# Six weight buffers spread over offsets modulo 128 bytes in SBUF

## The chip, the cores and the metric

The kernel runs on one core of a Trainium2 chip. The metric is the device time of one execution in microseconds. The time before is a median of 919.14 us over three runs (918.66 to 919.76).

## The reference, cut to what matters

The kernel computes one layer of a streaming-encoder block in float32 for 512 tokens of width 1024: a combined input projection, sliding-window attention, gated linear attention, a gated mix, cross-attention to 256 memory tokens, and a SwiGLU feed-forward block of inner width 2816.

```python
h = _rms(x, norm_mix_w)
proj = h @ w_in                      # attention q, k, v; GLA q, k, v, g, gate rank; branch gates
...
merged = g_a * (o_a @ w_attn_o) + g_b * (o_g @ w_gla_o)
x = x + merged @ w_mix_o
x = x + _memory_xattn(_rms(x, norm_mem_q_w), _rms(mem, norm_mem_kv_w), w_mem_q, w_mem_kv, w_mem_o)
x = x + (silu(hf @ w_gate) * (hf @ w_up)) @ w_down      # hf = _rms(x, norm_ffn_w)
out = _rms(x, norm_final_w)
```

What costs time is matrix products with weights of 83 MB in all, which are read from HBM once.

## The kernel before, in words

Every weight matrix comes in units of 128 partitions by up to 1024 columns of float32. `unit` (line 110) loads a unit by a DMA on SP's queue into a tile R, and `split` (line 95) makes two tiles of it: the upper part H, by a cast on ACT (line 97), and the lower part L = R - H, by a subtraction on DVE (line 98). Each of R, H and L has three buffers of 4096 bytes a partition, which take turns from unit to unit, so there are three for the upper and three for the lower part. Activations stand in the same way as pairs `xh`, `xl` (`weighted`, line 231), `oh`, `ol`, `mh`, `ml`, `ah`, `al` and so on, each 512 columns, 2048 bytes a partition.

A product is taken as three matmuls (`prod3`, line 122): H with `xh`, H with `xl`, L with `xh`. Two loops do nearly all of them:

- `block` (line 125): a piece of 128 columns (512 bytes a partition) of H or L is the stationary operand, and 512 tokens of an activation are the moving one. All gates, queries, output projections and the whole feed-forward part go this way. A unit gives eight pieces, so 24 matmuls.
- `tokens` and `token_terms` (lines 257 and 268): 128 tokens of an activation are stationary and a slice of H or L moves. It is 512 columns wide for the GLA's values and gates, and 328 for the columns of `w_tg` (TGW, line 31), with two slices in one unit; the second of these begins 328 x 4 = 1312 bytes into the tile, which is 32 modulo 128.

In the profile a matmul is named output<-moving,stationary, so `mm<-xh,H` is one of `block` and `mm<-H,xh` one of `token_terms`.

Tiles are placed in pools that fill SBUF from the left and the right end. The tile `edge` (line 50) is 96 bytes of padding at the right end. With it, H, L, R and all activation tiles begin at 0 modulo 128 bytes; some small tiles (`ident`, `ones`, `alr`, norm scalars) do not. The pool `wp` of R, H and L is the second from the left, behind `cp`, which holds the constants.

A scheduler sets the order of instructions on each engine from dependences and its own estimates of durations; in the attention part PE's order is written out by hand. Engines work through their rows in order, and semaphores tie them together. At the start, the first projection is computed while x arrives chunk by chunk: `load`, `chunk` and `keys` (lines 294 to 302) bring a chunk of x, make `xh` (ACT) and `xl` (DVE) of it and multiply it with the keys' weights (tile `o`), and `Norm.add` squares it (ACT, `sq`) and sums it (DVE, `acc_n`, line 205). `Norm.finish` then multiplies `acc_n` with `ones` on PE (`t<-ones,acc_n`).

Of the kernel before, what the change touches and what calls it, by code (L numbers as in the profile page):

```python
# [11 lines left out]
F32 = mybir.dt.float32  # L12
F32R = mybir.dt.float32r
# [7 lines left out]
P = 128  # L21
# [13 lines left out]
def build(tc, a, out):  # L35
# [3 lines left out]
    def pool(name, bufs=1, side=None, space=None):  # L39
        kw = {"name": name, "bufs": bufs, "reuse_waits": "tile"}  # L40
        if side is not None:
            kw["side"] = side
        if space is not None:
            kw["space"] = space
        return tc.tile_pool(**kw)

    cp = ctx.enter_context(pool("cp"))
# [3 lines left out]
    wp = ctx.enter_context(pool("wp"))  # L51
# [7 lines left out]
    def uniq(s):  # L59
        names[0] += 1  # L60
        return f"{s}_{names[0]}"
# [41 lines left out]
            )  # L103

    def unit_tiles():
        return [
            wp.tile([P, 1024], dt, tag=tag, bufs=3, name=uniq(tag)) for tag, dt in (("R", F32), ("H", F32R), ("L", F32R))
        ]

    def unit(src):  # L110
        n = src.shape[-1]
        r, h, lo = unit_tiles()
        nc.sync.dma_start(r[:, :n], src)
        split(h[:, :n], lo[:, :n], r[:, :n])
        return h, lo
# [34 lines left out]
    nc.gpsimd.memset(edge, 0.0)  # L150
    ident = cp.tile([P, P], F32, name="ident")
    make_identity(nc, ident)
    ones = cp.tile([P, P], F32, name="ones")
    nc.gpsimd.memset(ones, 1.0)

    def small(name, shape, src):
# [74 lines left out]
    def weighted(x, w, k):  # L231

        h = xwp.tile([P, S], F32R, tag="xw", bufs=16, name=uniq("xh"))
        lo = xwp.tile([P, S], F32R, tag="xw", bufs=16, name=uniq("xl"))
        split(h, lo, x, w[:, k : k + 1])
        return h, lo
# [495 lines left out]
    for t in range(NT):  # L732
# [9 lines left out]
        r = cp.tile([P, 4], F32, name=f"rr{t}")  # L742
# [43 lines left out]
    for j in range(KC):  # L786
# [7 lines left out]
        h = mg2.tile([P, S], F32R, name=f"mh{j}")  # L794
        lo = mg2.tile([P, S], F32R, name=f"ml{j}")
# [11 lines left out]
    for k in range(KC):  # L807
        if k % 2 == 0:
            two = f(xwp.tile([P, S], F32R, tag="xw", bufs=16, name=uniq("mem")))
        r = two[:, (k % 2) * NM : (k % 2 + 1) * NM]  # L810
# [5 lines left out]
    for k in range(KC):  # L816
# [3 lines left out]
        h = mep.tile([P, NM], F32R, name=f"eh{k}")  # L820
        lo = mep.tile([P, NM], F32R, name=f"el{k}")
# [8 lines left out]
    for j in range(KC):  # L830
# [6 lines left out]
        h, lo = weighted(x, wq_w, j)  # L837
# [151 lines left out]
    for u in range(2):  # L989
        h4, l4 = unit(a["w_mem_o"][u])  # L990
        for i in range(4):
# [9 lines left out]
            h, lo = weighted(res[j], wf_w, j)  # L1001
# [132 lines left out]
```

## Time and profile before

| | |
|---|---|
| median of three runs | 919.14 us |
| the profiled execution, its own time | 919.91 us |
| its span, first to last instruction | 918.1 us |
| PE busy | 901.2 us, 98% |
| DVE busy | 557.4 us, 61% |
| ACT busy | 426.5 us, 46% |
| granted TensorE clock, mean | 0.995 |

The record of a matmul with 512 columns is about 390 ns long, and in the feed-forward part the next one starts 227 ns after it, so records overlap. So the busy share says that PE is never empty, and not how fast it goes. The pace is read from the starts of matmuls that follow one another. [...]

### The profile page before, as it was taken

The numbers are of one execution on the slowest core, as the hardware profiler recorded it, in microseconds if no ns is written. First come the engines' busy times: TensorE is split into PE (matmuls) and PEld (weight loads), VectorE is DVE, ScalarE is ACT, GpSimd is POOL, SyncE is SP. The second block draws the span as 40 slices with busy tenths as digits, with TensorE's granted clock in tenths as the row PEclk, the third lists the DMA queues.
The fourth block names the chain that finished last, engine by engine and source line by source line (L and its number), as shares of the span: only waits on it lengthen the run. The fifth ranks groups of instructions, "written<-read, shape, count | busy, mean of one in ns | idle before, by whom it ended". The sixth has DMA issues, their size and how long they took to land.

```text
span 918.1 us, 11424 instructions
## 1 busy us (share of the span) xinstructions
PE 901.2 (98%) x4318; PEld 746.7 (81%) x4318; DVE 557.4 (61%) x1104; ACT 426.5 (46%) x760; POOL 7.0 (1%) x30
## 2 busy tenths in 40 slices
PE   8999999999999999999999999999999999999995
PEld 6898888887888787778888778888888888888885
DVE  6777888777343959966766996444444444323323
ACT  7576574556333838463445864223332233222220
POOL 1000000000000000000000000000000000000001
PEclk9999999999999999999999999999999999999998
DMA  7232221222232031425432222232222322323212
GB/s 249 92 115 70 69 70 69 70 69 69 92 96 89 23 115 48 143 86 161 114 115 92 70 89 95 94 107 99 92 92 92 106 100 86 104 86 103 87 41 92
DMA packets 29415, 86.11 MB, mean 94 GB/s; under 512 B 4048, under 2 KB 7760, under 8 KB 29360
## 3 DMA queue, kind: packets, MB, share of 16 engines
q1 hardware_dynamic: 29216, 85.37, 28.9%
q8 instruction: 34, 0.56, 0.2%
q14 instruction: 21, 0.17, 0.1%
q10 hardware_dynamic: 144, 0.00, 0.0%
HBM read 83.27 MB, written 2.10 MB: 93 GB/s over the span
## 4 chain that ended last, share of the span: by engine, by line
PE 89%; DVE 6%; ACT 3%; DMA 1%; issue 1%; SPq 0%; DVEq 0%; ACTq 0%
PE mm L79 80%; PE s L79 3%; PE o L79 3%; PE t L79 1%; DVE L L98 1%; PE t L545 1%; ACT pm L93 1%; DMA R<-in_w_tg 1%; PE mm L545 1%; ACT H L97 1%; DVE sl L98 1%; DVE on L747 1%; DMA x<-in_xT 0%; PE t L758 0%; DVE st L706 0%
## 5 line engine op out<-in xcount | busy, mean ns | idle before, releaser
L97 ACT CAST H<-R 128x1024 fp32r<-128x1024 f32 (+2 forms) x155 | 156.8, 1013 | 326.1 <-PE mm L79 247.0
L98 DVE TENSOR_TENSOR L<-R,H 128x1024 fp32r<-128x1024 f32 (+2 forms) x155 | 181.8, 1174 | 93.9 <-ACT H L97 93.5
L79 PE MATMUL mm<-xl,H 128*128 128x512 f32 x592 | 232.3, 392 | 0.0
L79 PE MATMUL mm<-xh,L 128*128 128x512 f32 x592 | 232.1, 392 | 0.0
L79 PE MATMUL mm<-xh,H 128*128 128x512 f32 x592 | 230.6, 390 | 0.0
L79 PEld LDWEIGHTS mm<-xh,H 128*128 128x128 f32 x592 | 111.2, 188 | 22.5
L79 PEld LDWEIGHTS mm<-xl,H 128*128 128x128 f32 x592 | 111.2, 188 | 22.1
L79 PEld LDWEIGHTS mm<-xh,L 128*128 128x128 f32 x592 | 111.3, 188 | 21.7
L79 PE MATMUL mm<-ah,H 128*128 128x512 f32 (+1 forms) x198 | 72.5, 366 | 0.0
L79 PE MATMUL mm<-ah,L 128*128 128x512 f32 (+1 forms) x198 | 72.4, 366 | 0.0
L79 PE MATMUL mm<-al,H 128*128 128x512 f32 (+1 forms) x198 | 72.4, 365 | 0.0
L79 PE MATMUL mm<-H,xh 128*128 128x512 f32 (+1 forms) x192 | 70.3, 367 | 0.0
L79 PE MATMUL mm<-L,xh 128*128 128x512 f32 (+1 forms) x192 | 70.3, 366 | 0.0
L79 PE MATMUL mm<-H,xl 128*128 128x512 f32 (+1 forms) x192 | 70.1, 365 | 0.0
L1024 DVE TENSOR_TENSOR t2k<-t2k,mm 128x512 f32<-128x512 f32 x22 | 15.0, 687 | 68.3 <-PE mm L79 67.7
L93 ACT ACTIVATE p<-sm,nm,sc 128x256 f32<-128x256 f32 (+1 forms) x64 | 36.3, 569 | 25.4 <-DVE es L519 20.3
L1022 DVE TENSOR_TENSOR t2k<-mm,rb_n 128x512 f32<-128x512 f32 x22 | 15.1, 691 | 44.9 <-PE mm L79 43.0
L79 PEld LDWEIGHTS mm<-al,H 128*128 128x128 f32 x198 | 37.3, 189 | 6.1
L79 PEld LDWEIGHTS mm<-ah,H 128*128 128x128 f32 x198 | 37.3, 189 | 6.0
L79 PEld LDWEIGHTS mm<-ah,L 128*128 128x128 f32 x198 | 37.3, 189 | 6.0
L79 PEld LDWEIGHTS mm<-L,xh 128*128 128x128 f32 x192 | 36.1, 188 | 5.5 <-DVE L L98 0.6
L79 PEld LDWEIGHTS mm<-H,xh 128*128 128x128 f32 x192 | 36.3, 189 | 5.1 <-issue 0.2
(300 smaller groups left out, 1365.7 us busy)
## 6 DMA issues: line engine op xcount, KB each, us to landing
R<-in_w_fg SPq DMA_DIRECT2D x22, 512.0 KB, 3.2
R<-in_w_fu SPq DMA_DIRECT2D x22, 512.0 KB, 3.3
R<-in_w_gate SPq DMA_DIRECT2D x16, 512.0 KB, 3.3
R<-in_w_fd SPq DMA_DIRECT2D x16, 512.0 KB, 3.5
x<-in_xT SPq DMA_DIRECT2D x16, 256.0 KB, 3.5
R<-in_w_q SPq DMA_DIRECT2D x8, 512.0 KB, 3.5
R<-in_w_attn_o SPq DMA_DIRECT2D x8, 512.0 KB, 3.3
R<-in_w_vg SPq DMA_DIRECT2D x8, 512.0 KB, 3.3
```

Of the source, the lines that this page charges most:

```text
L79: nc.tensor.matmul(o, lhsT=lhsT, rhs=rhs, start=start, stop=stop)
L93: last_table[0] = nc.scalar.activation(*args, **kw)
L97: nc.scalar.copy(out=hi, in_=src)
L98: nc.vector.tensor_tensor(out=lo, in0=src, in1=f(hi), op=ALU.subtract)
L545: nc.tensor.transpose(out=pt[:, i * P : (i + 1) * P], in_=prs[i // 2][:, i % 2, b * P : (b + 1) * P], identity=ident)
L747: nc.vector.scalar_tensor_tensor(out=on[t][:, vs], in0=on[t][:, vs], scalar=r[:, h : h + 1], in1=glaw, op0=ALU.mult, op1=ALU.mult)
L1022: nc.vector.tensor_tensor(out=t, in0=pg, in1=n2.b, op=ALU.mult)
L1024: nc.vector.tensor_tensor(out=t, in0=t, in1=pu, op=ALU.mult)
```

## The change

```diff
     def unit_tiles():
-        return [
-            wp.tile([P, 1024], dt, tag=tag, bufs=3, name=uniq(tag)) for tag, dt in (("R", F32), ("H", F32R), ("L", F32R))
-        ]
+        r = wp.tile([P, 1024], F32, tag="R", bufs=3, name=uniq("R"))
+        i = wturn[0] = (wturn[0] + 1) % 3
+        h = wp.tile([P, 1024 + 8], F32R, tag=f"H{i}", bufs=1, name=uniq("H"))
+        lo = wp.tile([P, 1024 + (24 if i == 2 else 8)], F32R, tag=f"L{i}", bufs=1, name=uniq("L"))
+        return r, h[:, 8:1032], lo[:, 8:1032]
+
+    wturn = [-1]
...
-    ones = cp.tile([P, P], F32, name="ones")
+    ones = cp.tile([P, 32], F32, name="ones")
```

Each H and L tile gets 8 columns (32 bytes) more in front, and its data begin behind them. The tiles lie one behind the other as H0, L0, H1, L1, H2, L2, each 4128 bytes long (32 x 128 + 32) but the last, which is 4192. So they begin at 0, 32, 64, 96, 0 and 32 modulo 128, and their data at 32, 64, 96, 0, 32 and 64. Together they are 256 bytes longer than before, which is twice 128; `ones` is 384 bytes shorter, three times 128. So every other tile keeps its offset modulo 128. R is as it was. The three buffers of each part take turns as before, and every wait on a buffer stays; only two columns of `ones` were ever read.

No instruction is added or removed. Its memset being shorter, `ones` shifts the scheduler's estimates on POOL a little, and some rows at the kernel's start change places; after the first projection all rows stand as before on every engine. ACT at the start, where x's chunks 4 to 7 (`x_4` to `x_7`) and the last two units of `w_tg` and the second half of `w_k` (`R_214`) arrive, before:

```order
L97 CAST H_215<-R_214 128x512
L100 ACTIVATE xh_257<-x_4_81,wk 128x512
L199 ACTIVATE sq_278<-x_4_81 128x512
L100 ACTIVATE xh_262<-x_5_82,wk 128x512
L97 CAST H_267<-R_266 128x656
L100 ACTIVATE xh_285<-x_6_83,wk 128x512
L199 ACTIVATE sq_281<-x_5_82 128x512
L97 CAST H_295<-R_294 128x656
L100 ACTIVATE xh_290<-x_7_84,wk 128x512
```

ACT at the same place, now:

```order
L100 ACTIVATE xh_257<-x_4_81,wk 128x512
L97 CAST H_215<-R_214 128x512
L100 ACTIVATE xh_262<-x_5_82,wk 128x512
L204 ACTIVATE sq_278<-x_4_81 128x512
L97 CAST H_267<-R_266 128x656
L100 ACTIVATE xh_285<-x_6_83,wk 128x512
L204 ACTIVATE sq_281<-x_5_82 128x512
L100 ACTIVATE xh_290<-x_7_84,wk 128x512
L97 CAST H_295<-R_294 128x656
```

Two casts of weights have gone behind a chunk of x, and one square behind a chunk. DVE follows, before:

```order
L98 TENSOR_TENSOR L_216<-R_214,H_215 128x512
L101 SCALAR_TENSOR_TENSOR xl_258<-x_4_81,wk,xh_257 128x512
L205 TENSOR_TENSOR acc_n_124<-acc_n_124,sq_278 128x512
L101 SCALAR_TENSOR_TENSOR xl_263<-x_5_82,wk,xh_262 128x512
L98 TENSOR_TENSOR L_268<-R_266,H_267 128x656
L205 TENSOR_TENSOR acc_n_124<-acc_n_124,sq_281 128x512
L101 SCALAR_TENSOR_TENSOR xl_286<-x_6_83,wk,xh_285 128x512
L98 TENSOR_TENSOR L_296<-R_294,H_295 128x656
L101 SCALAR_TENSOR_TENSOR xl_291<-x_7_84,wk,xh_290 128x512
L205 TENSOR_TENSOR acc_n_124<-acc_n_124,sq_306 128x512
```

and now:

```order
L101 SCALAR_TENSOR_TENSOR xl_258<-x_4_81,wk,xh_257 128x512
L98 TENSOR_TENSOR L_216<-R_214,H_215 128x512
L101 SCALAR_TENSOR_TENSOR xl_263<-x_5_82,wk,xh_262 128x512
L210 TENSOR_TENSOR acc_n_124<-acc_n_124,sq_278 128x512
L98 TENSOR_TENSOR L_268<-R_266,H_267 128x656
L101 SCALAR_TENSOR_TENSOR xl_286<-x_6_83,wk,xh_285 128x512
L210 TENSOR_TENSOR acc_n_124<-acc_n_124,sq_281 128x512
L101 SCALAR_TENSOR_TENSOR xl_291<-x_7_84,wk,xh_290 128x512
L98 TENSOR_TENSOR L_296<-R_294,H_295 128x656
L210 TENSOR_TENSOR acc_n_124<-acc_n_124,sq_306 128x512
```

`xl` now stands ahead of the sum `acc_n` and of the lower parts beside it. On PE the three rows `mm_126<-H_267,xh_257`, `mm_126<-H_267,xl_258` and `mm_126<-L_268,xh_257` have gone behind the last two of the keys, `o_125<-xl_291,H_215` and `o_125<-xh_290,L_216`. SP's rows, the DMAs, stand as before.

## Rows read from the trace of the kernel before

**Rows 1.** The profile's page: busy time of each engine, and the chain's shares by engine.

```profile
PE 901.2 (98%) x4318; PEld 746.7 (81%) x4318; DVE 557.4 (61%) x1104; ACT 426.5 (46%) x760; POOL 7.0 (1%) x30
...
PE 89%; DVE 6%; ACT 3%; DMA 1%; issue 1%; SPq 0%; DVEq 0%; ACTq 0%
```

**Rows 2.** The chain that ended last: start us, length us, engine, line, count.

```profile
563.52 333.00 PE mm L79 x1500
```

**Rows 3.** Two stretches: length, busy us and count by engine, granted clock, DMA share, GB/s.

```profile
60.00:240.00 180.00, 180.00 (x904) 149.19 (x903) 139.48 (x400) 110.68 (x251) 0.32 (x1) 1.00 0.23 76
...
565.00:885.00 320.00, 320.00 (x1413) 265.08 (x1412) 134.31 (x158) 96.37 (x118) 0.00 (x0) 1.00 0.30 94
```

**Rows 4.** Timeline in the feed-forward part: start us, length us, engine, line, operation.

```profile
600.13 0.39 PE L79 MATMUL mm<-xh,H 128*128 128x512 f32 x1
...
600.37 1.22 DVE L98 TENSOR_TENSOR L<-R,H 128x1024 fp32r<-128x1024 f32 x1
...
604.22 1.06 ACT L97 CAST H<-R 128x1024 fp32r<-128x1024 f32 x1 [3.11 <-PE mm L79]
...
605.57 0.39 PE L79 MATMUL mm<-xh,H 128*128 128x512 f32 x1
```

**Rows 5.** PE's groups by form: line, operation, count, busy us, mean ns, idle before.

```profile
L79 PE MATMUL mm<-xh,H 128*128 128x512 f32 x592 | 230.6, 390 | 0.0
L79 PE MATMUL mm<-ah,H 128*128 128x512 f32 x154 | 59.9, 389 | 0.0
...
L79 PE MATMUL mm<-H,xh 128*128 128x512 f32 x128 | 50.3, 393 | 0.0
...
L79 PE MATMUL mm<-ogh,H 128*128 128x512 f32 x64 | 24.5, 394 | 0.0
...
L79 PE MATMUL mm<-H,xh 128*128 128x328 f32 x64 | 20.0, 314 | 0.0
```

**Rows 6.** Timeline of token_terms over w_tg: every third matmul, H or L moving.

```profile
48.62 0.31 PE L79 MATMUL mm<-H,xh 128*128 128x328 f32 x1
...
49.08 0.31 PE L79 MATMUL mm<-H,xh 128*128 128x328 f32 x1
...
49.52 0.31 PE L79 MATMUL mm<-H,xh 128*128 128x328 f32 x1
...
49.97 0.31 PE L79 MATMUL mm<-H,xh 128*128 128x328 f32 x1
...
50.42 0.31 PE L79 MATMUL mm<-H,xh 128*128 128x328 f32 x1
```

**Rows 7.** Timeline of the last product, 256 columns wide: two matmuls with 23 between.

```profile
889.04 0.28 PE L79 MATMUL mm<-ah,L 128*128 128x256 f32 x1
...
891.92 0.28 PE L79 MATMUL mm<-ah,L 128*128 128x256 f32 x1
```

**Rows 8.** DVE's and ACT's largest groups by form, columns as in rows 5.

```profile
L98 DVE TENSOR_TENSOR L<-R,H 128x1024 fp32r<-128x1024 f32 x136 | 166.1, 1222 | 89.1 <-ACT H L97 88.7
...
L97 ACT CAST H<-R 128x1024 fp32r<-128x1024 f32 x136 | 142.8, 1052 | 295.2 <-PE mm L79 223.3 <-issue 71.6
```

**Rows 9.** DMA issues from 0 to 30 us: count, KB each, us to landing.

```profile
x<-in_xT SPq DMA_DIRECT2D x8, 256.0 KB, 4.4
```

**Rows 10.** Timeline of the kernel's start.

```profile
8.50 0.90 SPq L295 DMA_DIRECT2D x<-in_xT  x2
...
12.29 0.62 ACT L97 CAST H<-R 128x512 fp32r<-128x512 f32 x1 [1.15 <-DMA R<-in_w_k]
...
17.24 0.74 ACT L97 CAST H<-R 128x656 fp32r<-128x656 f32 x1 [0.25 <-DMA R<-in_w_tg]
...
18.44 0.50 PE L79 MATMUL o<-xl,H 128*128 128x512 f32 x1 [0.92 <-DVE xl L101]
...
21.10 0.69 DVE L205 TENSOR_TENSOR acc_n<-acc_n,sq 128x512 f32<-128x512 f32 x1 [0.47 <-ACT sq L199]
...
21.94 1.02 PE L79 MATMUL t<-ones,acc_n 128*128 128x2 f32 x8
```

## The prediction, made before the changed kernel ran

> **What bounds the kernel now.** I read the page first: PE is busy for 901.2 of 918.1 us, and the chain that ended last is 89% PE [rows 1]. The chain's longest piece is 333.00 us of matmuls without a break [rows 2]. So the kernel is as fast as PE steps from one matmul to the next, and DVE and ACT matter only where PE waits for them.
>
> The pace is read next. In the feed-forward part two matmuls `mm<-xh,H` start at 600.13 and 605.57; 24 steps lie between them, as one unit of weights has 24 matmuls, so a step is 5.44 / 24 = 226.7 ns [rows 4]. The whole stretch says the same: 1413 matmuls in 320.00 us are 226.5 ns each, at a granted clock of 1.00, which is the 2.4 GHz level [rows 3]. At that clock 512 columns take 512 / 2.4 = 213.3 ns. So each step is 13.3 ns, or 32 column times, longer than its columns. Two other widths show the same excess: twelve steps of 328 columns take 50.42 - 48.62 = 1.80 us, 150.0 ns each [rows 6], where the columns take 136.7; and 24 steps of 256 columns take 2.88 us, 120.0 ns each [rows 7], where they take 106.7. What these 13.3 ns are, no row says. They are the only thing on the path that a buffer's place could change, and that is the whole question.
>
> **The change part by part.** Nothing is added or removed, so each item is a change of duration or of order. *H and L as stationary operands* (`block`). The rows count 592 + 154 + 3 x 64 groups of three matmuls with 512 moving columns (`ogh` in the row; `oh` and `mh` have as many) [rows 5], so 2814 steps. The moving tiles stay at 0 modulo 128 bytes. The pieces of H and L are 512 bytes long, so all pieces of one tile have their tile's offset: 0 in all of them before, and now 32 and 96 for two thirds and one third of H, 64 and 0 for L. Three causes for the 13.3 ns can be told apart by what the offset does: a fixed cost of changing weights (nothing), a collision of the weight load with the moving stream in a bank that is chosen by the low address bits (a change of either sign), and a cost for rows that begin off a boundary (a loss). The trace of before holds one natural experiment on it, the next item.
>
> *H and L as moving operands* (`token_terms`). Of the 328-column slices every second one begins at 32 modulo 128, against a stationary operand at 0. In [rows 6] the slices alternate: three steps from 48.62 and three from 49.52 are at offset 0 and take 0.46 + 0.45 = 0.91 us, the three from 49.08 and from 49.97 are at offset 32 and take 0.44 + 0.45 = 0.89 us. That is 151.7 against 148.3 ns a step, which is one printed digit, and the twelve together take exactly 12 x 150.0, that is columns plus 32, just as the widths whose operands all lie at 0. If offset 32 paid, the sum should have come out below; if it cost, above. I read it as no effect, with a bound of 1.7 ns a step (half of the difference) on either side. A distance of 32 bytes between the two operands also covers H1 as a stationary operand (weights at 96, stream at 0), and L1 stays at 0. Distances of 64 (L0, L2) and 96 (H0, H2) are in no row that is paced by columns. By the two seen I take 0 for them too, and the bound goes into the rivals. Sum: 0 us.
>
> *DVE and ACT.* `L<-R,H` takes 1222 ns and `H<-R` 1052 ns [rows 8]. In the feed-forward part DVE is busy for 134.31 and ACT for 96.37 of 320 us [rows 3], so per unit (5.44 us) for 2.3 and 1.6 us. If each subtraction took half as long again, 0.6 us more, the 3.1 us of slack would hide it. In the attention part (60 to 240 us) DVE is busy for 139.48 of 180 us and 904 matmuls run [rows 3], at 24 a unit no more than 38 units; 0.6 us each would be 23 us of the 40 us that DVE has free there. Also, neither engine gains anything for the end if it gets faster. 0 us.
>
> *The start.* Here rows change places. ACT took the keys' last unit at 12.29, having waited 1.15 us for it to land, and `x_4` behind it [rows 10]. Now `x_4` comes first. It was issued at 8.50 [rows 10], and chunks of x land after 4.4 us [rows 9], so at about 12.9; ACT then starts 12.9 - 12.29 = 0.6 us later than before, and the sums `acc_n` behind it on DVE by up to as much. Some of it comes back, since ACT had 0.25 us of waiting before the last cast of `w_tg` [rows 10]. On the other side, `xl` of chunk 6 now stands ahead of a sum, and PE's 0.92 us of waiting for it at 18.44 shrinks. But that gain ends at the next wait: `t<-ones,acc_n` started at 21.94, and the last sum ended at 21.79 (21.10 + 0.69) [rows 10], so PE can't go through there more than 0.1 us earlier whatever it saves ahead of it. Between -0.1 and +0.6 us; I take +0.3, as the landing that moved is the nearer row. The smaller memset of `ones` lies on POOL, which is busy for 7.0 us in all [rows 1], and is hidden.
>
> Sum: the profiled execution's 919.91 us (span 918.1 and 1.8 around it) + 0 + 0 + 0.3 = 920.2. That execution was 0.8 above the median of 919.14, and the result will be a median, so 919.4 us.
>
> **The rivals.** *Faster: the 13.3 ns are a collision that the equal offsets make.* Weights and stream are read at the same time, and now both begin at the same place modulo 128. Moving the weights to 32, 64 and 96 would free the stream. For it: the excess is the same for 256, 328 and 512 columns, as it would be if each weight load cost a fixed number of reads. Against it: offset 32 in [rows 6]. At the bound from there it gives 1.7 ns for 2814 + 3 x 128 = 3198 steps of 512 columns [rows 5], so 5.4 us: 914.0. If the whole excess went it would be 42.6 us: 877. [...] Chance 0.16.
>
> *Slower: a moving row that begins off a 128-byte boundary costs one piece more.* 2048 bytes at offset 0 are 16 pieces of 128 bytes, and at 32, 64 or 96 they touch 17. 32 columns of 4 bytes are just 128 bytes, so the price of a piece would be one more 13.3 ns. It falls in `token_terms` over the GLA's values and gates: 384 steps [rows 5], of which eight ninths use a buffer off 0 (H in two of three matmuls, always off 0; L in one, off 0 in two of three buffers), so 341 x 13.3 = 4.5 us: 923.9. For it: the 328-column rows say nothing on it, as 1312 bytes touch 11 pieces at offset 0 and at 32. It decides from half a piece on. Against it: no row shows any price of an offset. As stationary operands the pieces are covered, the weight loads being busy for 265.08 of 320 us [rows 3] beside the stream. [...] Collisions at the unseen distances of 64 and 96 would end on this side as well; they concern two thirds of 3198 steps, and 1.7 ns each are 3.6 us: 923.0. Chance of both 0.18.
>
> *The change doesn't do what it says.* Sizes and paddings add up to the offsets named, and the tiles around keep theirs, so only if the real granule were larger than 128 bytes would all stay alike; that gives 919.4 too, and is part of the forecast.
>
> **How the numbers follow.** No measurable change has 0.66, faster 0.16, slower 0.18. About 0.2%, or 1.8 us, is what a measurement of this kernel can tell from no change; the start alone, -0.1 to +0.6 us, stays inside. The likeliest case alone reaches from 918.0 to 921.0, by the spread of the three runs and the start. The range goes to the prices of the two rivals at their bounds, 914.0 and 923.9, which holds the forecast and about half of each rival, 0.83.
>
> **What would show it.** If I am right, the step in the feed-forward part stays at 226.7 ns in all three turns of the buffers, and the 328-column steps at 150.0. The faster rival would show as a shorter step in units of some buffers, repeating every three units; the slower one as a step of about 240 ns for `mm<-H,xh` with 512 columns, with `block` unchanged. In the start, `t<-ones,acc_n` should come between 21.8 and 22.5. I would be wrong above all if the pace depends on a distance of 64 or 96 bytes, on which the trace has no row.

## The result, and the profile after

The changed kernel takes 932.75 us, the median of four runs (932.18 to 933.45), against 919.21 us for the kernel before on the same chip. The ratio is 1.0148, with a 95% interval of 1.0130 to 1.0165. So it is slower by 13.5 us, where I forecast 919.4 us and no measurable change; the time lies above the whole range (914.0 to 923.9).

The profiled execution of the changed kernel took 932.18 us, its span is 930.4 us, and its mean granted clock 0.996 (0.995 before). From its page, the busy times and the chain's shares by engine:

```profile
PE 915.1 (98%) x4318; PEld 746.5 (80%) x4318; DVE 556.9 (60%) x1104; ACT 425.8 (46%) x760; POOL 6.8 (1%) x30
...
PE 92%; DVE 3%; ACT 2%; DMA 1%; issue 1%; SPq 0%; DVEq 0%; ACTq 0%
```

PE is busy for 13.9 us more than in [rows 1] with the same 4318 matmuls, DVE and ACT are as they were, and the chain has moved from DVE and ACT to PE. So PE did not wait longer: its work became longer. The stretch 565 to 885 us by windows (us, then PE, PEld, DVE, ACT, POOL busy with counts, granted clock, DMA share, GB/s) says how:

```profile
565.00:885.00 320.00, 319.94 (x1385) 258.88 (x1385) 134.13 (x165) 93.61 (x114) 0.00 (x0) 1.00 0.28 93
```

PE is full and at the same clock as in [rows 3], but 1385 matmuls start in 320 us instead of 1413: 231.0 ns a step instead of 226.5. The chain's pieces (start, length, engine, line, count), of the changed kernel:

```profile
228.72 73.00 PE mm L79 x313
...
569.19 340.48 PE mm L79 x1500
```

and the piece of the kernel before that answers to the first of them:

```profile
227.66 71.18 PE mm L79 x313
```

The long feed-forward piece of [rows 2] has grown from 333.00 to 340.48 us, so by 7.5 of the 12.3 us that the span grew; the piece of 313 matmuls ahead of it by 1.8. The rest lies in other stages. The timeline shows that the loss goes by buffers. These are four first matmuls of a unit, 24 steps apart, with the buffer that H has in turn: 0, 1, 2, and 0 again.

```profile
599.67 0.39 PE L79 MATMUL mm<-xh,H 128*128 128x512 f32 x1
...
605.22 0.39 PE L79 MATMUL mm<-xh,H 128*128 128x512 f32 x1
...
610.77 0.39 PE L79 MATMUL mm<-xh,H 128*128 128x512 f32 x1
...
616.37 0.39 PE L79 MATMUL mm<-xh,H 128*128 128x512 f32 x1
```

A unit takes 5.55, 5.55 and 5.60 us, where [rows 4] had 5.44, and the next three take the same again. That is 231.3, 231.3 and 233.3 ns a step. One more thing can be read here. H0 and H2, and L0 and L2, lie at the same offsets modulo 128 (32 and 64), yet their units differ by 2 ns a step. So what counts is not the place modulo 128 alone.

### The profile page after: what moved, and what is told of

Its sections match the earlier page's. It is cut to its first block, busy times and chain, and to the rows that moved or that the text cites. A ratio compares the mean times of both kernels' runs of the same rounds, so it can differ in the third digit from the quotient of the medians.

```text
span 930.4 us, 11424 instructions
## 1 busy us (share of the span) xinstructions
PE 915.1 (98%) x4318; PEld 746.5 (80%) x4318; DVE 556.9 (60%) x1104; ACT 425.8 (46%) x760; POOL 6.8 (1%) x30
## 4 chain that ended last, share of the span: by engine, by line
PE 92%; DVE 3%; ACT 2%; DMA 1%; issue 1%; SPq 0%; DVEq 0%; ACTq 0%
PE mm L79 83%; PE o L79 3%; PE s L79 3%; PE t L79 1%; PE t L550 1%; ACT pm L93 1%; PE mm L550 1%; DMA x<-in_xT 1%; DVE L L98 0%; DMA R<-in_w_k 0%; PE t L763 0%; ACT H L97 0%; DVE sl L98 0%; ACT th L97 0%; DVE mkl L260 0%
## 5 line engine op out<-in xcount | busy, mean ns | idle before, releaser
L79 PE MATMUL mm<-xh,L 128*128 128x512 f32 x592 | 234.9, 397 | 0.0
L79 PE MATMUL mm<-xh,H 128*128 128x512 f32 x592 | 233.1, 394 | 0.0
```

The lines of the kernel that those rows point to most:

```text
L79: nc.tensor.matmul(o, lhsT=lhsT, rhs=rhs, start=start, stop=stop)
```

## Experiments

Three causes were open: the distance in bytes between the two operands that PE reads; a start off a boundary as such; and something else that the change moved (the order at the start, the tiles of activations on either side). In all that follows, *distance* is the address of the stationary operand's piece less that of the moving one. For the kernel and its variants it is that of `block`, where the weights are stationary.

**1. The changed layout with H and L put back to 0.** The order at the start and the shift of the left-hand tiles stay.

```diff
-        h = wp.tile([P, 1024 + 8], F32R, tag=f"H{i}", bufs=1, name=uniq("H"))
-        lo = wp.tile([P, 1024 + (24 if i == 2 else 8)], F32R, tag=f"L{i}", bufs=1, name=uniq("L"))
-        return r, h[:, 8:1032], lo[:, 8:1032]
+        h = wp.tile([P, 1024], F32R, tag=f"H{i}", bufs=1, name=uniq("H"))
+        lo = wp.tile([P, 1024 + (64 if i == 2 else 0)], F32R, tag=f"L{i}", bufs=1, name=uniq("L"))
+        return r, h, lo[:, 0:1024]
```

> The changed kernel with its order of rows and its places of all other tiles, but H and L themselves at 0 modulo 128 again (256 bytes of padding stand behind L2). H and L are now 256 or 384 bytes (modulo 512) away from the activations, instead of 0. Theory 1, distance: a step's time depends on the distance in bytes between the start of the moving stream and the start of the weights that are loaded beside it, and a distance of 0 is the good one. If only the distance modulo 128 counts, 919 us and a step of 226.7 ns in the feed-forward part; if a larger modulus counts, slower, up to 932.8. Theory 2, boundary: an operand that starts off a 128-byte boundary costs more: 919 us. Theory 3, something else that the change moved (the rows at the start, the other tiles by 128 and 384 bytes): 932.8 us and steps of 231 to 233 ns.

It took 921.29 us, 1.0023 times the kernel before (1.0014 to 1.0033). The changed order is not the cause. The chain's pieces:

```profile
226.73 72.18 PE mm L79 x313
...
564.65 332.97 PE mm L79 x1500
```

The feed-forward piece is back at 333 us. The small loss of 2 us has a place: the piece of 313 matmuls, 72.18 us against 71.18, and one of 153, 35.60 against 34.79, where `oh` and `ogh` are multiplied; the mean step of the 153 is 35.60 / 153 = 232.7 ns, where it was 227.4. The change shifts the tiles on the left by 128 bytes, weights included, and not those on the right. `oh`, `ogh` and `omh` stand on the right, so 432 steps have a distance of 128 here where they had 0. About 2 us over 432 steps is 5 ns each, much as the steps of the changed kernel pay. Multiples of 128 are not all alike.

**2. Everything at 32.** The kernel before, with 32 bytes put ahead of `wp` and the padding at the right end made 32 bytes shorter, so that weights and activations all lie at 32 modulo 128, at distance 0.

```diff
-    edge = ctx.enter_context(pool("ep", side="right")).tile([P, 24], F32, name="edge")
+    edge = ctx.enter_context(pool("ep", side="right")).tile([P, 16], F32, name="edge")
+    shift = ctx.enter_context(pool("shp")).tile([P, 8], F32, name="shift")
...
+    nc.gpsimd.memset(shift, 0.0)
```

> The kernel before, with every tile behind the constants, H, L, R and all activations, 32 bytes further: every operand starts at 32 modulo 128, and all distances stay 0. Theory 1, distance: 919 us, a step of 226.7 ns. Theory 2, boundary: slower; with one price per operand off a boundary at least as slow as the changed kernel (932.8 us), in which only H and L are off. Theory 3 has no reason for a change: 919 us.

It took 919.39 us, ratio 1.0003 (0.9993 to 1.0013), and its feed-forward piece 332.99 us. A start off a boundary costs nothing by itself. Only the distance is left.

**3. The distance alone.** A kernel that leaves the whole block out: PE runs 24 matmuls for each setting, at chosen offsets of weights (`st`) and stream (`mv`), and its output is a copy of x. From 30 to 330 us no DVE or ACT instruction runs, and DMA moves 1 GB/s. The loop, simplified to its float32 settings:

```python
def run(name, s, m, cols=512, ...):        # s, m: offsets of weights and stream in bytes
    for i in range(24):
        st = w[:, s // 4 + i // 3 * P : s // 4 + i // 3 * P + P]
        mv = xs[i // 3][:, m // 4 : m // 4 + cols]
        nc.tensor.matmul(o[:, :cols], lhsT=st, rhs=mv, ...)
```

> Not the block of the reference: PE alone, with nothing else running, does 24 matmuls with 24 weight loads per setting, and the output is a copy of x. The settings: the stationary operand 0 to 496 bytes from a 512-byte boundary in steps of 16 (and 4, 8, 12) with the stream at 0 (st); the stream at 32 to 480 in steps of 32 with the weights at 0 (mv); both at the same offset (both); 32, 64 and 96 stationary columns instead of 128 at offsets 0 and 32 (w); 256 moving columns (c256); bf16 operands (bfst). Theory 1, distance: 226.7 ns a step at st0 and in all of both, 229 to 236 at other distances, and mv at an offset the same as st at minus that offset. Theory 2, boundary: both as slow as st and mv. If the excess of 32 columns over the 512 comes from the reads of the weight load, it shrinks with the stationary columns (8, 16 and 24 at 32, 64 and 96) and is smaller for bf16, which has half the bytes; if it is a fixed price of changing weights, it stays 13.3 ns at any width. If steps at some distance take less than 226.7 ns, there is a kernel that beats both.

From its timeline, one row for each setting (start, length, engine, line, operation, output<-moving,stationary, count); the step is the time to the next row's start, divided by 24. Starts are printed to 0.01 us, so a step read in this way is good to about 0.4 ns:

```profile
26.57 5.60 PE L58 MATMUL st0x<-x,w 128*128 128x512 f32 x24
32.01 5.61 PE L58 MATMUL st16x<-x,w 128*128 128x512 f32 x24
37.46 5.75 PE L58 MATMUL st32x<-x,w 128*128 128x512 f32 x24
43.05 5.76 PE L58 MATMUL st48x<-x,w 128*128 128x512 f32 x24
...
93.33 5.66 PE L58 MATMUL st192x<-x,w 128*128 128x512 f32 x24
98.82 5.76 PE L58 MATMUL st208x<-x,w 128*128 128x512 f32 x24
...
110.02 5.62 PE L58 MATMUL st240x<-x,w 128*128 128x512 f32 x24
115.48 5.60 PE L58 MATMUL st256x<-x,w 128*128 128x512 f32 x24
120.92 5.61 PE L58 MATMUL st272x<-x,w 128*128 128x512 f32 x24
...
204.38 5.77 PE L58 MATMUL mv32x<-x,w 128*128 128x512 f32 x24
209.99 5.67 PE L58 MATMUL mv64x<-x,w 128*128 128x512 f32 x24
...
288.12 5.62 PE L58 MATMUL both32x<-x,w 128*128 128x512 f32 x24
293.57 5.64 PE L58 MATMUL both64x<-x,w 128*128 128x512 f32 x24
...
309.99 5.71 PE L58 MATMUL w32st0x<-x,w 128*32 128x512 f32 x24
315.53 5.87 PE L58 MATMUL w32st32x<-x,w 128*32 128x512 f32 x24
...
359.88 5.34 PE L58 MATMUL bfst32x<-xb,wb 128*128 128x512 bf16 x24
365.06 5.34 PE L58 MATMUL bfst64x<-xb,wb 128*128 128x512 bf16 x23
370.24 5.34 PE L58 MATMUL bfst96x<-xb,wb 128*128 128x512 bf16 x24
```

At distance 0 a step is 5.44 / 24 = 226.7 ns, the kernel's own pace, and at 16 it is 227.1. At 32 it is 5.59 / 24 = 232.9 ns, and it stays between 231.7 and 234.2 up to 160. At 176 it is 230.0, at 192 228.8, at 208 and 224 again 233.3, and at 240 (227.5) and 256 (226.7) the cheap place has come back. The second half, up to 496, repeats the first, so the period is 256 bytes. Moving the stream instead costs as much (`mv32x`, 233.8 ns), and the sign counts: with the stream moved by 64 the step is 229.2 ns, the sweep's at 192 and not its 232.9 at 64. Moving both by 32 costs nothing (227.1). So PE alone pays for the distance between its two operands, modulo 256, and no other engine or DMA is needed for it. With bfloat16 a step is 5.18 / 24 = 215.8 ns at 32 and at 64, and at 0 it is 216.3 (5.19 us). Fewer stationary columns do not make the step shorter: with 32 of them it is 230.8 ns at distance 0, with 64 and with 96 it is 230.0. So the part of the expectation by which the 13.3 ns over the columns would shrink with the columns of the weight load did not come true.

**4 and 5. One common distance in the real kernel.** All six buffers as before, but behind a pad, so that every weight lies 32, or 192, bytes off every activation modulo 256. All activations stay where they were. Against the kernel before, shortened:

```diff
-    ones = cp.tile([P, P], F32, name="ones")
+    ones = cp.tile([P, 32], F32, name="ones")
...
+        if not padded:
+            padded.append(wp.tile([P, 40], F32, tag="front", bufs=1, name="front"))   # 192: [P, 16]
+        h = wp.tile([P, 1024], F32R, tag="H", bufs=3, name=uniq("H"))
+        lo = wp.tile([P, 1024], F32R, tag="L", bufs=3, name=uniq("L"))
+        if len(padded) == 1:
+            padded.append(wp.tile([P, 56], F32, tag="back", bufs=1, name="back"))     # 192: [P, 80]
```

> Kernel before with H and L in three buffers each as before, one behind the other, but the whole block of six moved by a pad in front of it, so that every weight tile, of H and of L and in all three turns, lies 32 bytes off the activations modulo 256 (before: 0). All activations keep their addresses; ones is cut to 32 columns as in the changed kernel. Theory (the distance modulo 256 sets the step, as in the sweep): the feed-forward step goes from 226.7 to the sweep's 233.4 ns in all three turns alike, and 3198 steps of 512 columns times 6.7 ns are 21.4 us, so about 940.6 us, slower than the changed kernel although only one distance is in use. Rival (the price comes from the turn, buffers that lie differently from one unit to the next): one common distance costs nothing, 226.7 ns and 919 us.

> The same with a pad by which all six weight buffers lie 192 bytes off the activations modulo 256. Theory: the sweep's step at this distance is 228.9 ns, 2.2 more than at 0; for 2814 steps of block that is 6.2 us, and the 384 steps with the weights moving stand at the sweep's row of a stream moved by 192, 233.3 ns, for another 2.5 us, so about 928 us, and a feed-forward step of 228.9 ns in all turns. Rival (any distance but 0 costs the same in this kernel, whatever the sweep of PE alone says): the step of the changed kernel, 231 to 233 ns, and 933 to 940 us. Rival (the turn): 919 us.

They took 936.23 us (ratio 1.0188, 1.0173 to 1.0203) and 925.13 us (1.0067, 1.0050 to 1.0083). The feed-forward pieces of the chain, first at 32, then at 192:

```profile
571.33 342.40 PE mm L79 x1500
```

```profile
565.90 336.00 PE mm L79 x1500
```

Against 333.00 us [rows 2] these are 9.4 and 3.0 us more. The piece of before holds 1434 steps of 512 columns (three groups of 324 for `xh` and `xl`, three of 154 for `ah` and `al`) and, at its end, 66 of 256. The sweep's prices, 6.3 to 6.7 ns (its rows at 32 and 288) and 2.1 ns, make 9.0 to 9.6 and 3.0 us for the 1434. With 120.0 ns for each of the 66 [rows 7], the mean step of the 1434 is 233.2 ns at 32 and 228.8 at 192, as in the sweep, while the buffers take turns as before. So the turn of the buffers isn't what costs, and not every distance costs the same. The whole times came out 4 and 3 us below what I expected: the program's 3267 steps of 512 columns (3198 by the prediction's rows, which leave out 48 with `omh` and 21 with the keys) pay less than the full price outside the feed-forward part. From 60 to 240 us, for instance, 894 matmuls start at distance 32 and 904 before [rows 3], 1.1% fewer and not 2.9%. Narrow matmuls stand between those of 512 columns there; what of the price goes for that, and what in waits that shrank, I did not take apart.

**6. The changed kernel's own sequences, on PE alone.** As in 3, with the order H, H, L of `prod3` and the distances of the three buffers: 32 and 64, 96 and 128, 160 and 192. The calls, written out and shortened:

```python
seq("buf0x", [(32, 0), (32, 0), (64, 0)] * 24)      # (weights, stream); buf1x: 96, 96, 128; buf2x: 160, 160, 192
seq("lonlyx", [(0, 0), (0, 0), (32, 0)] * 24)       # honlyx: 32, 32, 0
seq("c328pairs", ([(0, 0)] * 3 + [(0, 32)] * 3) * 4, cols=328)
```

> PE alone, matmuls without the rest of the block, weights and stream at chosen offsets; the output is only a copy of x. allzero and eachzero: 226.7 ns a step. buf0x, buf1x, buf2x take the changed kernel's order of three (H, H, L) at the distances that its three buffers have in the feed-forward part (32 and 64, 96 and 128, 160 and 192), and turns takes the three in rotation. Theory (nothing but addresses counts): they show the kernel's own steps, 231.3, 231.4 and 233.2 ns, without DVE, ACT or a DMA beside them; rival (other engines' accesses make part of it): they show the sweep's mixture, about 233.3, 234.0 and 231.7. honlyx and lonlyx: two thirds and one third of the steps at distance 32; if each step pays alone, 231.1 and 228.9 ns. own and next tell which pair counts: in own, each matmul's stream is off its own weights and level with the weights loaded for the next one; in next, it is level with its own and off the next ones. Theory (the load of the next weights runs beside the stream): own stays at 226.7, next goes to 233; if own weights count, the other way round. c rows: steps of 256 to 480 columns, at 0 and at 32. If the price belongs to the weight load (128 columns long in every row), it is 6.7 ns at each width; if to the stream's length, it shrinks with the columns. c328mv32x and c328pairs repeat the slices of 328 columns that my prediction read as no effect: 150.0 ns if that reading was right for this width, 156 if the row was misread.

```profile
26.32 16.49 PE L58 MATMUL allzero<-x,w 128*128 128x512 f32 x72
42.65 16.81 PE L58 MATMUL buf0x<-x,w 128*128 128x512 f32 x72
59.30 16.82 PE L58 MATMUL buf1x<-x,w 128*128 128x512 f32 x72
75.96 16.97 PE L58 MATMUL buf2x<-x,w 128*128 128x512 f32 x72
92.77 50.26 PE L58 MATMUL turns<-x,w 128*128 128x512 f32 x216
142.87 16.85 PE L58 MATMUL honlyx<-x,w 128*128 128x512 f32 x72
159.55 16.95 PE L58 MATMUL lonlyx<-x,w 128*128 128x512 f32 x72
176.34 16.49 PE L58 MATMUL eachzero<-x,w 128*128 128x512 f32 x72
...
307.71 3.76 PE L58 MATMUL c328mv32x<-x,w 128*128 128x328 f32 x24
311.31 3.76 PE L58 MATMUL c328pairs<-x,w 128*128 128x328 f32 x24
```

From start to start, 72 steps take 16.33 us at distance 0, and 16.65, 16.66 and 16.81 us in the three buffers: 226.8, then 231.3, 231.4 and 233.5 ns. The changed kernel's units took 231.3, 231.3 and 233.3. Addresses alone make the whole of its feed-forward loss; the mean, 232.0, is 5.2 ns over 226.8, and 1434 such steps are 7.5 us, as measured. A prediction by averaging the sweep's steps at these distances (about 233.3, 234.0 and 231.7) would have the third buffer as the cheapest, and it is the dearest. With L alone off (`lonlyx`) one step in three is misplaced, and yet the mean is 16.79 / 72 = 233.2 ns, more than with H alone off, 231.7, where it is two in three.

Two more kinds of row were to tell which pair of operands sets the price: streams level with the next weights and off their own, or the other way round. They gave 230.4 and 231.9 ns at 32, 230.6 and 234.0 at 96, 230.0 and 228.3 at 128. Both cost, so this stayed open. Slices of 328 columns with the stream moved by 32 take 3.60 / 24 = 150.0 ns: for this width the reading in my prediction was right. Moving the weights by 32 at that width costs 2.5 ns (152.9 against 150.4).

**7 and 8. Only H off, only L off, in the real kernel.** As experiment 4, with pads that put only one of the two at distance 32 (for L: front 32 columns, 8 between H and L, and 56 behind; for H: front 40, and 56 between).

```diff
+        if len(padded) == 1:
+            padded.append(wp.tile([P, 8], F32, tag="mid", bufs=1, name="mid"))        # H off: [P, 56]
         lo = wp.tile([P, 1024], F32R, tag="L", bufs=3, name=uniq("L"))
```

> The kernel with every weight at distance 32, but only the three buffers of H so; the three of L go back to distance 0. Two thirds of the steps are off. If every step pays for its own distance, the feed-forward step is 226.7 + 6.7 x 2/3 = 231.1 ns, and two thirds of the 17.5 us of that kernel remain: about 930.5 us. If steps disturb their neighbours as in the sequence honly on PE alone (16.68 us for 72 steps, 231.7 ns), the step is 231.7 ns and the time about 932 us.

> The same with only the three buffers of L at distance 32 and H at 0, so that one step in three is off. If every step pays for its own distance: 226.7 + 6.7 / 3 = 228.9 ns, and about 925 us. If steps disturb their neighbours as in the sequence lonly on PE alone (16.79 us for 72 steps, 233.2 ns): 233.2 ns, and nearly all of the 17.5 us, about 935.5 us, so that one third of the misplaced steps costs more than two thirds of them do in the run with H alone.

They took 932.46 us (ratio 1.0145, 1.0128 to 1.0162) and 935.39 us (1.0175, 1.0160 to 1.0190). The feed-forward pieces, H off, then L off:

```profile
568.60 340.26 PE mm L79 x1500
```

```profile
570.26 342.39 PE mm L79 x1500
```

As on PE alone: a third of the steps misplaced costs 9.4 us there, as much as all of them misplaced, and two thirds cost 7.3. That every step pays for its own distance is refuted.

**9. Single misplaced steps, and other widths.** PE alone again; in `oneof8x` one step in eight is at 32 and seven at 0, 48 steps in each row.

> PE alone, as in the run of sequences. The c rows have steps of 352 to 512 columns at distances 0 and 32, 48 steps each. If the price is one of 512 columns alone (their 2048 bytes are a whole number of 256-byte periods), c504 and c508 show none and c512 6.7 ns; if it grows with width, it rises from c448 on. The oneof rows have one step in n at distance 32 and the others at 0. If a single misplaced step costs a fixed time of its own, 6.7 ns, the mean falls as 226.7 + 6.7 / n, so 230.0 at n = 2 and 226.9 at 24; if it disturbs the steps behind it for long, the mean stays near 233 for small n and falls later.

```profile
125.66 11.07 PE L58 MATMUL c504st0x<-x,w 128*128 128x504 f32 x48
136.57 11.19 PE L58 MATMUL c504st32x<-x,w 128*128 128x504 f32 x48
147.60 11.09 PE L58 MATMUL c508st0x<-x,w 128*128 128x508 f32 x48
...
169.56 11.07 PE L58 MATMUL c512st0x<-x,w 128*128 128x512 f32 x48
180.46 11.36 PE L58 MATMUL c512st32x<-x,w 128*128 128x512 f32 x48
191.66 11.44 PE L58 MATMUL oneof2x<-x,w 128*128 128x512 f32 x48
202.94 11.35 PE L58 MATMUL oneof3x<-x,w 128*128 128x512 f32 x48
214.13 11.28 PE L58 MATMUL oneof4x<-x,w 128*128 128x512 f32 x48
225.25 11.20 PE L58 MATMUL oneof6x<-x,w 128*128 128x512 f32 x48
236.29 11.16 PE L58 MATMUL oneof8x<-x,w 128*128 128x512 f32 x48
247.29 11.12 PE L58 MATMUL oneof12x<-x,w 128*128 128x512 f32 x48
```

At `oneof8x` the mean is 11.00 / 48 = 229.2 ns, 2.5 over 226.7, so one misplaced step costs 8 x 2.5 = 20 ns. One in six costs 20 ns, one in four 20, one in three 19, one in two 17. If all are misplaced alike, each costs 6.7. The form I had first, a fixed time for each, holds from one in twelve (20 ns) to one in three; its size was wrong, three times the 6.7 ns that a step pays where all are misplaced alike. And 20 ns in every third step is 6.7 ns a step, which is why L alone costs as much as H and L together. The trace has the single starts too: in `oneof12x` the step ahead of a misplaced one takes 235 ns, the misplaced one itself 228, the two behind it 233 and 231, and the others 226 or 227. So nearly all of the 20 ns falls on its neighbours. And a distance that is cheap when all lie alike isn't so for a single step: one in eight at 192 makes a mean of 229.4 ns, at 64 of 229.2, again some 20 ns each (one in three, 231.0 and 231.3, costs 13).

The width matters as well: 6.3 ns in these rows at 512 columns, but 2.5 at 504 (229.8 against 227.3), 2.1 at 508, 3.1 at 496, nothing at 480 (experiment 6), 3.5 at 400, and at 256 columns the steps at 32 are faster, 117.9 against 119.6. I had expected either none below 512 or a rise with the width, and neither came: there is no simple rule in these, beyond that 512 columns pay most among the widths tried. Level steps don't follow one rule either. A step of 504 columns takes 227.3 ns, as long as one of 512, so 17 ns over its columns, where 512 columns have 13.3, if both are counted at the 0.417 ns a column by which the steps of 256, 328 and 512 columns grow [rows 4, 6, 7].

## Why the prediction was wrong, step by step

**What bounds the kernel: right.** PE's step sets the time, and the cause of the loss is a longer step. DVE and ACT were costed at 0, which holds. The groups of the changed kernel that answer to [rows 8]:

```profile
L98 DVE TENSOR_TENSOR L<-R,H 128x1024 fp32r<-128x1024 f32 x136 | 166.0, 1221 | 91.6 <-ACT H L97 91.3
L97 ACT CAST H<-R 128x1024 fp32r<-128x1024 f32 x136 | 142.3, 1048 | 307.0 <-PE mm L79 235.9 <-issue 70.2 <-ACT on L732 0.3
```

1221 and 1048 ns, against 1222 and 1052.

**"H and L as stationary operands … 0 us": the step that failed.** The term put at 0 measured 5.2 ns a step and 7.5 us in the feed-forward part alone. It rested on the 328-column slices of [rows 6], "I read it as no effect, with a bound of 1.7 ns a step". The reading of the rows was right. In the changed kernel these steps still go at their old pace, 24 of them in 51.94 - 48.33 = 3.61 us, 150.4 ns each:

```profile
48.33 0.31 PE L79 MATMUL mm<-L,xh 128*128 128x328 f32 x1
...
51.94 0.31 PE L79 MATMUL mm<-L,xh 128*128 128x328 f32 x1
```

And experiment 6 has 150.0 ns for just this case. What failed was the transfer. The slices differ from the steps I priced in two ways: they are 328 columns wide and not 512, and it is the stream that is moved and not the weights. Either is enough to change the price: with 328 columns, moving the weights costs 2.5 ns and moving the stream none; with 512 columns, moving the stream costs 7. The 1.7 ns bound became 4.6 to 6.7 ns. The same excess of 32 columns at three widths had persuaded me that widths behave alike. It says nothing on what misplaced operands cost at each of them, and by experiment 9 it isn't even the same at all widths with level operands. The 2.4 GHz with which I counted columns stands in no row, but the rate does: from 256 to 512 columns the step grows by 106.7 ns [rows 4, 7], 0.417 ns a column or 2.4 columns a ns, and the 150.0 ns at 328 lie on the same line [rows 6]. So the 13.3 ns are an estimate from these three steps.

**"Distances of 64 and 96 are in no row … By the two seen I take 0 for them too."** The gap was named, and named as what would make me wrong. But the loss doesn't sit there alone. The prediction counted from the weights to the stream, so its covered 32 is a stream 32 bytes further than its weights, or, by the modulus of 128, weights at 96. At 512 columns the first takes 233.8 ns (`mv32x`) and the second 234.2 (the sweep's row at 96): both cost as much as the rest.

**The modulus.** I took the change's own 128 for the chip's. By it "L1 stays at 0", and H0 and H2 are equals. In bytes modulo 256, L1 lies at 128, where the sweep has 233.3 ns, and H2 at 160 where H0 lies at 32. I did write that the granule might be larger, and concluded that then all would stay alike; with 256 the opposite holds, since the shift of 128 between the left and the right tiles, which I passed as keeping every tile's offset, costs some 2 us by itself (experiment 1).

**The slower rival.** Its mechanism, one more piece for a moving row off a boundary, is refuted by experiment 2: 919.39 us with every row off the boundary. The clause behind it, a loss at unseen distances, is the kind of thing that happened (whether by collisions, no run shows), but priced with the bound from the 328-column slices on two thirds of the steps, 3.6 us. With the measured mean of 5.2 ns on all 3198 steps that I counted, it would have been 16.6 us and 936: near the 932.75 measured, which is lower because the price outside the feed-forward part is smaller. So the chance of 0.18 went to a case of the right sign whose term was small by a factor of four. **The faster rival** looked for a price of equal offsets; at 512 columns they are the cheapest of those tried (226.7 ns at 0, 232.9 at 32). What the 13.3 ns are that remain at distance 0 stays open. In bfloat16 the same columns, with loads of 128 columns too, step in 215.8 ns. And float32 loads of 32 columns leave the step at 230.8, though narrow loads are shorter: in the kernel before, those of 16 columns take 88 ns (`t<-ident,alr`) where those of 128 take 188 (`mm<-xh,H`).

**The start: outside what I stated, its sign not decidable.** I expected `t<-ones,acc_n` between 21.8 and 22.5. It came at 21.11, against 21.94 before:

```profile
21.11 1.02 PE L79 MATMUL t<-ones,acc_n 128*128 128x2 f32 x8
```

That is a gain of 0.8 us where I had a loss of 0.3. The landing of `x_4`, which I put at about 12.9, came earlier: ACT took it at 12.16. But the kernels of experiments 2, 4, 5, 7 and 8 keep the old order at the start, and have `t<-ones,acc_n` at 21.23, 22.13, 21.25, 20.85 and 21.84; that of experiment 1 has the new order, and 21.15. One profiled execution differs from another by more than the term; it was no term to be read from one trace.

## What to carry to other kernels

Where PE's steps set the time, the place of a tile is a matter of its distance from the operand it meets: in these float32 matmuls with 512 columns, weights and stream that begin at the same place modulo 256 bytes cost least (226.7 ns a step at 0 and 256, 232.9 at 32), and one misplaced step in three costs as much as all (342.39 and 342.40 us for the feed-forward piece at distance 32). So padding or a shrunk constant that moves one side of SBUF against the other should be a multiple of 256 bytes, and this holds for every buffer of a tile that takes turns. For other widths and for bfloat16 the runs show a smaller price (2.5 ns at 504 columns), none (480 columns, bfloat16), or a gain (1.7 ns at 256). The natural experiment in the trace here carried only to its own width and its own operand (150.0 ns at 328 columns with the stream moved); a run of PE alone with 24 steps a setting answers such a question directly.

## What the runs showed of the hardware that I had not expected

- The step of a float32 matmul of 512 columns depends on the distance between its operands with a period of 256 bytes: 226.7 ns at 0 and 256, 227.1 at 16, 227.5 at 240, 228.8 at 192, 230 to 234 at the other multiples of 16 below 256. At 8 and 12 it costs something too, 230.8 and 230.0. Nothing else has to run beside it.
- The price of a misplaced step depends on its neighbours: 6.7 ns when all lie alike, 20 ns for one among level ones, and most of these fall on the steps beside it (235, 233 and 231 ns in `oneof12x`).
- It depends on the width: 6.3 to 6.7 ns at 512 columns, 2.1 to 3.1 at 496 to 508, nothing at 480, 3.5 at 400, and a gain of 1.7 ns at 256.
- bfloat16 at 512 columns: 216 ns at distances of 0, 32 and 64 alike.
- Where all lies at distance 0, an offset of 32 modulo 128 costs nothing (919.39 us). No kernel of this study was faster than the one before.
